# A two-layer encoder on one core: timeline-driven scheduling, TensorE in source order, later turns, all weight remainders on VectorE

## The chip, the cores and the metric

The kernel runs on one core of one Trainium2 chip. The metric is the device time of one execution in microseconds. The core has TensorE (PE in the rows; its weight loads are PEld), VectorE (DVE), ScalarE (ACT), GpSimd (POOL) and SyncE (SP), each with its own queue of instructions; they meet at semaphores.

## What is computed

x is 256 tokens by 1024 channels in float32, and there are two layers. In each, with RMSNorm ahead of every sublayer:

```python
for l in range(DEPTH):
    h_res = h_res + 0.5 * swiglu(rmsnorm(h_res, ffn1_norm[l]), ffn1_w_gate[l], ffn1_w_up[l], ffn1_w_down[l])
    z = rmsnorm(h_res, mix_norm[l]) @ w_in[l]
...
    y_att = dilated_attention(zq, zk, zv, q_norm[l], k_norm[l], biases)
    y_pool = pool_mixer(zp, pool_w[l], pool_scale[l])
    y_rec = hgrn2_bidirectional(hq, hi, hff, hfb, hg, lb_all[0, l], lb_all[1, l], hgrn_norm[l])
    h_res = h_res + jnp.concatenate([y_att, y_pool, y_rec], axis=-1) @ w_out[l]
    h_res = h_res + 0.5 * swiglu(rmsnorm(h_res, ffn2_norm[l]), ffn2_w_gate[l], ffn2_w_up[l], ffn2_w_down[l])
```

The attention has 8 heads of 64, the pooling 4 groups, and the recurrence (a gated scan over the tokens in both directions) 4 heads of 64. The FFN is 2816 wide.

## The kernel before

**Weights.** All weights stream in one after the other as 328 halves of 128x1024 float32 (512 KB each), each by one DMA on SP into one of 4 `stage` buffers. A product of float32 accuracy is made of three fp32r matmuls (`mm3`, `mm3t`, L164 to L176): every operand is split into a rounded part and a remainder. For a half `split_part` (L142) makes `whi` with an ACT copy and `wlo` with a subtraction; the subtraction runs on DVE, or on POOL for the 35 halves of the two mixers that `POOL_HALVES` lists (`on_pool`, L153). `ahead` (L158) starts the split of the half that lies LOOK = 4 further on. Activations are split alike by `split` (L256) and, for the normalised x, by `parts` (L270) into `xh` and `xl`.

**Stages.** There are six: FFN, mixer, FFN, twice. An FFN (`ffn`, L322) has 11 blocks; a block multiplies by 4 halves of gate and up (`gate_up`, L189), makes `h` with ACT and DVE, turns it with four TensorE transposes (`hp`, L352), and multiplies the block before by 2 halves of the down matrix (`down`, L238). At the end of a stage the four quarters of the new x are added (L371), squared on ACT for the norm (`squares`, L278), and turned by transposes (`turn`, L289, tiles `xps`) for the next stage; `to_stage` (L374) turns three at once and holds the last one back as `pending`, which `late_turn` (L183) issues inside the next stage.

**Mixer.** `mixer` (L449) first makes the gates `ga` and `gb` (`proj_pair`, 4 halves), then runs a list of steps by name, `ORDER[l]` (L48). `c:0` to `c:19` are the halves of the input projection (two for `hq`, four each for `q`, `k` and `zh`, two for `hg`, four for `v`). `ga`, `gb`, `uv` prepare the recurrence's `U` and `W`; its levels are `mm:m` (small TensorE matmuls, `lev`, L541), `put:m` (their results into `A`, for m below 32 a DVE copy by a mask, L566) and `up:m` (DVE multiplies U and W up to the next level, L520). `mm:m` needs the `U` and `W` that `up:m` left. `ns`, `nq`, `nk` scale and turn q and k, `sc`, `tr`, `pv` are the attention, `band` and `pool` the pooling, `join`, `rec`, `rnorm` end the recurrence, and `o:` are the four parts of the output projection (`wo`, 2 halves each). `head_rs` (L601) sums squares over a head with two matmuls `hss` for `rnorm`. Short-lived tiles of 128x512 come from a pool `t2` of T2 = 10 buffers.

**Order.** The tile scheduler orders the instructions of each engine by its priorities, which follow the source; only SP is in source order. So TensorE's order is the scheduler's.

**Start.** The kernel takes x twice: as it is and transposed (`xt_in`). The transposed copy lands in `self.xt0` by four DMAs on SP, between which the first half of weights comes in two parts; `body` makes `xh` and `xl` from it with no transpose. `setup` (L390) loads the masks and the bias table and builds the attention bias; it stands at block 4 of the first FFN.

Of the kernel before, what the change touches and what calls it, by code (L numbers as in the profile page):

```python
# [8 lines left out]
F32 = mybir.dt.float32  # L9
# [3 lines left out]
ALU = mybir.AluOpType  # L13
# [40 lines left out]
    ),  # L54
    (
# [7 lines left out]
POOL_HALVES = ((3, 4, 5, 7, 8, 9, 12, 16, 20, 22, 24, 25, 27, 28, 29, 31), (2, 5, 6, 7, 8, 12, 16, 18, 19, 20, 21, 23, 24, 25, 26, 27, 28, 29, 31))  # L63
T2 = 10
# [6 lines left out]
class Trunk:  # L71
    def __init__(self, ctx, tc, x_in, xt_in, wall, prm_in, rel_in, cst_in, cst2_in, msk_in, band_in, y_out):
# [18 lines left out]
        self.pending = None  # L91
# [11 lines left out]

        self.xt0 = self.bias[:, 0]
        self.cp.tile([P, 16], F32, name="pad0")
        xr = xt_in.rearrange("p (k t) -> p k t", k=KC)
# [3 lines left out]
        for j in range(4):  # L110
            if j < 2:
                q = slice(j * HALF // 2, (j + 1) * HALF // 2)
                nc.sync.dma_start(w0[:, q], wall[0][:, q])
            nc.sync.dma_start(self.xt0[:, 2 * j:2 * j + 2, :], xr[:, 2 * j:2 * j + 2, :])
        self.feed_dma(2)
        self.prm_in, self.cst_in = prm_in, cst_in
        self.ident = self.cst[:, K_ID:K_ID + P]
        nc.scalar.dma_start(self.ident, cst_in[:, K_ID:K_ID + P])
        nc.scalar.dma_start(self.x, x_in.rearrange("p (t d) -> p t d", t=2))
# [22 lines left out]
    def split_part(self, i, c0, c1):  # L142
# [40 lines left out]
    def late_turn(self):  # L183

        if self.pending is not None:
            self.pending()
            self.pending = None

    def gate_up(self, i0, gu, mid=None):  # L189

        for q in range(4):
            if q == 1:
                self.late_turn()
            if q == 2 and mid is not None:
                mid()
            self.ahead(i0 + q)
# [125 lines left out]
    def ffn(self, stage, post):  # L322
# [67 lines left out]
    def setup(self, after):  # L390
# [562 lines left out]
```

## Time and profile before

| | us |
|---|---|
| median of 3 runs | 1041.35 (1040.72 to 1043.3) |
| the profiled execution | 1040.81 |
| its span in the trace | 1039.0 |
| TensorE busy, share of the span | 1004.4 (97%) |
| VectorE busy | 585.0 (56%) |
| ScalarE busy | 538.8 (52%) |
| GpSimd busy | 88.3 (8%) |

Some 1.8 us of the profiled execution lie outside its span. A busy engine is one with an instruction in flight; a waiting instruction is not busy, and the idle time ahead of it is shown in brackets with what ended it. The six stages follow one another at 201.76, 333.67, 521.44, 708.60 and 849.72 us, where the first matmul of the next stage starts; the two mixers are the stretches from 201.76 to 333.67 and from 708.60 to 849.72.

### The profile page before, as it was taken

To read this page: it belongs to the slowest core of one execution; us is meant where nothing else is said; L and a number is where in the kernel's file an instruction comes from. 1 tells how busy PE (TensorE), PEld (TensorE's weight loads), DVE (VectorE), ACT (ScalarE), POOL (GpSimd) and SP (SyncE) were. 2 spreads that over 40 slices of the span, in tenths; PEclk is the share of its full clock that TensorE was granted. 3 is DMA by queue.
4 is the path that set the end of the run, shared out by engine and by line. 5 is a ranking of instruction groups with operands and counts; after the bars stand their busy time and mean duration, and the time that the engine had idled before them with its cause. 6 is when DMAs were issued, how large, how long until landed. Compare 5 with 4: busy or idle time off the path is not lost.

```text
span 1039.0 us, 14421 instructions
## 1 busy us (share of the span) xinstructions
PE 1004.4 (97%) x5682; PEld 826.2 (80%) x5682; DVE 585.0 (56%) x776; ACT 538.8 (52%) x774; POOL 88.3 (8%) x43
## 2 busy tenths in 40 slices
PE   6999999998999999999999999999889999999998
PEld 4878888886867888888878888889768678888886
DVE  5655555669835555555565555554977155555553
ACT  7544444684865544444564444447648555444442
POOL 0000000140230000000000000004132400000000
PEclk9999999999999999999999999999989999999999
DMA  7769655553334555555555555554523346555551
GB/s 265 245 219 329 234 188 193 165 163 123 103 122 136 179 192 182 186 192 188 185 168 187 190 185 186 195 185 138 165 83 102 102 147 196 184 185 189 194 186 58
DMA packets 50420, 182.20 MB, mean 175 GB/s; under 512 B 5768, under 2 KB 6024, under 8 KB 49968
## 3 DMA queue, kind: packets, MB, share of 16 engines
q1 hardware_dynamic: 48528, 174.09, 51.6%
q0 software_dynamic: 720, 4.21, 1.1%
q10 hardware_dynamic: 1104, 2.99, 0.8%
q8 instruction: 44, 0.72, 0.3%
q14 instruction: 24, 0.20, 0.1%
HBM read 180.20 MB, written 3.16 MB: 176 GB/s over the span
## 4 chain that ended last, share of the span: by engine, by line
PE 87%; DVE 6%; ACT 3%; issue 3%; DMA 1%; POOL 0%; SPq 0%; ACTq 0%; DVEq 0%; POOLq 0%
PE gu L175 15%; PE gu L176 15%; PE gu L174 15%; PE ya L174 8%; PE ya L176 8%; PE ya L175 8%; PE hp L352 2%; PE wo L174 2%; PE wo L175 1%; PE wo L176 1%; ACT whi L149 1%; DVE wlo L151 1%; PE xps L296 1%; DMA bias<-x_t 1%; PE lev L541 1%
## 5 line engine op out<-in xcount | busy, mean ns | idle before, releaser
L149 ACT ACTIVATE whi<-stage 128x1024 fp32r<-128x1024 f32 (+1 forms) x329 | 347.1, 1056 | 395.3 <-PE gu L176 202.3
L151 DVE TENSOR_TENSOR wlo<-stage,whi 128x1024 fp32r<-128x1024 f32 (+1 forms) x294 | 360.7, 1229 | 337.5 <-ACT whi L149 337.4
L174 PE MATMUL gu<-whi,xh 128*128 128x512 f32 x704 | 275.7, 392 | 8.0 <-ACT xh L274 5.7
L175 PE MATMUL gu<-wlo,xh 128*128 128x512 f32 x704 | 274.9, 391 | 0.5 <-DVE wlo L151 0.5
L176 PE MATMUL gu<-whi,xl 128*128 128x512 f32 x704 | 274.7, 390 | 0.0
L174 PEld LDWEIGHTS gu<-whi,xh 128*128 128x128 f32 x704 | 132.5, 188 | 37.5 <-ACT xh L274 5.7
L175 PEld LDWEIGHTS gu<-wlo,xh 128*128 128x128 f32 x704 | 132.7, 189 | 28.7 <-DVE wlo L151 1.4
L176 PEld LDWEIGHTS gu<-whi,xl 128*128 128x128 f32 x704 | 132.6, 188 | 27.7
L174 PE MATMUL ya<-whi,hi 128*128 128x512 f32 x352 | 141.2, 401 | 0.0
L151 POOL TENSOR_TENSOR wlo<-stage,whi 128x1024 fp32r<-128x1024 f32 x35 | 85.0, 2437 | 654.5 <-ACT whi L149 639.2
L176 PE MATMUL ya<-whi,lo 128*128 128x512 f32 x352 | 137.8, 391 | 0.0
L175 PE MATMUL ya<-wlo,hi 128*128 128x512 f32 x352 | 137.4, 390 | 0.0
L176 PEld LDWEIGHTS ya<-whi,lo 128*128 128x128 f32 x352 | 66.1, 188 | 14.3
L175 PEld LDWEIGHTS ya<-wlo,hi 128*128 128x128 f32 x352 | 66.3, 188 | 12.4
L174 PEld LDWEIGHTS ya<-whi,hi 128*128 128x128 f32 x352 | 66.2, 188 | 12.3
L345 ACT ACTIVATE g<-gu,rc 128x256 f32<-128x256 f32 x88 | 41.5, 475 | 47.4 <-PE gu L176 47.4
L346 DVE SCALAR_TENSOR_TENSOR h<-gu,rc,g 128x256 f32<-128x256 f32 x88 | 42.0, 481 | 23.7 <-ACT g L345 23.7
L260 DVE TENSOR_TENSOR lo<-hp,hi 128x512 fp32r<-128x512 f32 x44 | 30.1, 684 | 2.8 <-ACT hi L259 2.8
L259 ACT ACTIVATE hi<-hp 128x512 fp32r<-128x512 f32 x44 | 25.6, 581 | 2.7 <-PE hp L352 2.7
L541 PE MATMUL lev<-U,W 64*64 64x64 f32 x384 | 15.6, 237 | 11.4 <-DVE W L520 11.4
L352 PEld LDWEIGHTS hp<-cst,h 128*128 128x128 f32 x176 | 21.8, 139 | 5.7
L352 PE MATMUL hp<-cst,h 128*128 128x128 f32 x176 | 26.3, 272 | 0.0
(224 smaller groups left out, 1035.8 us busy)
## 6 DMA issues: line engine op xcount, KB each, us to landing
stage<-w_all SPq DMA_DIRECT2D x327, 512.0 KB, 3.5
skew<-drow POOLq DMA_DIRECT2D x1, 2048.0 KB, 12.1
bias<-skew POOLq DMA_DIRECT2D x2, 1024.0 KB, 10.3
bias<-x_t SPq DMA_DIRECT2D x4, 256.0 KB, 7.9
x<-x ACTq DMA_DIRECT2D x1, 1024.0 KB, 8.4
band<-band ACTq DMA_DIRECT2D x1, 1024.0 KB, 8.0
y_t<-x SPq DMA_DIRECT2D x4, 256.0 KB, 2.2
stage<-w_all SPq DMA_DIRECT2D x2, 256.0 KB, 4.7
```

The lines of the kernel that those rows point to most:

```text
L149: nc.scalar.activation(hi[:, s], st[:, s], AF.Copy)
L151: eng.tensor_tensor(lo[:, s], st[:, s], hi[:, s].bitcast(F32), op=ALU.subtract)
L174: nc.tensor.matmul(out, lhsT=ah, rhs=wh, start=start, stop=False, skip_group_check=True)
L175: nc.tensor.matmul(out, lhsT=ah, rhs=wl, start=False, stop=False, skip_group_check=True)
L176: nc.tensor.matmul(out, lhsT=al, rhs=wh, start=False, stop=stop, skip_group_check=True)
L259: self.nc.scalar.activation(hi, src, AF.Copy)
L260: self.nc.vector.tensor_tensor(lo, src, hi.bitcast(F32), op=ALU.subtract)
L296: nc.tensor.transpose(self.xps[k // 2][:, j % 2, tt * P:tt * P + P], self.x[:, tt, k * P:k * P + P], self.ident)
L345: silu = nc.scalar.activation(g2[:, tt, :], gu[tt][:, 0:256], AF.Silu, scale=r)
L346: nc.vector.scalar_tensor_tensor(h[:, tt, :], gu[tt][:, 256:512], r, g2[:, tt, :], op0=ALU.mult, op1=ALU.mult)
L352: nc.tensor.transpose(hp[:, f, tt * P:tt * P + P], h[:, tt, f * P:f * P + P], self.ident)
L541: nc.tensor.matmul(ps[d][e * 64:e * 64 + 64, hb * 64:hb * 64 + 64], lhsT=a, rhs=c, start=(hb == 0), stop=(hb == 7), skip_group_check=True)
```

## The change

1. The tile scheduler orders instructions with a simulated timeline (`schedule_with_timeline_sim`), and TensorE, like SP, is kept in source order.
2. `POOL_HALVES` and `on_pool` go: all subtractions for `wlo` are on DVE. 16 move in the first mixer and 19 in the second.
3. `ORDER` is rewritten: the levels are spread wider over the projections (in the first mixer `mm:2` from `c:6` to `c:7`, `mm:16` from `c:10` to `c:12`, `mm:128` from `c:13` to `c:15`), `rnorm` becomes `rn1` (squares and their split) and `rn2`, and `rec`, `rn1`, `rn2` come before the end of the projections. `ga`, `gb`, `uv` and `up` are given high priority.
4. `t2` has 16 buffers for 10; the `Kp` tag has one for two.
5. `to_stage` holds every turn back by one quarter.
6. The transposed copy of x is no longer an input. x comes by four DMAs on SP, 12 matmuls on a tile of ones stand at the start, and x is turned by 16 transposes, of which eight come in the second quarter of the first block; the squares come in its last quarter, and `look` grows from 0 to LOOK.
7. `setup` is cut in two: its loads stand at block 3, its computing at block 6.

```diff
-        "rnorm c:17 tr:6 tr:7 c:18 c:19 o:pool pv:0 pv:1 pv:2 o:rec pv:3 o:a0 o:a1 "
...
+        "c:14 mm:64 up:128 put:64 sc:2 tr:0 c:15 mm:128 put:128 join tr:1 sc:3 c:16 tr:2 band rec rn1 c:17 rn2 tr:3 tr:4 pool c:18 tr:5 tr:6 "
+        "c:19 tr:7 o:pool pv:0 pv:1 o:rec pv:2 pv:3 o:a0 o:a1 "
...
-T2 = 10
+FIRST = 400
+T2 = 16
...
-        eng = nc.gpsimd if self.on_pool(i) else nc.vector
-        eng.tensor_tensor(lo[:, s], st[:, s], hi[:, s].bitcast(F32), op=ALU.subtract)
-
-    def on_pool(self, i):
...
+        nc.vector.tensor_tensor(lo[:, s], st[:, s], hi[:, s].bitcast(F32), op=ALU.subtract)
...
-        self.feed_split(i + LOOK)
+        self.feed_split(i + self.look)
...
+            self.look = min(self.look + 1, LOOK)
...
+            if q == 3 and self.then is not None:
+                self.then()
+                self.then, self.look = None, LOOK
...
-            if b == min(4, NB - 1) and stage == 0:
-                self.setup(silu)
+            if b == 3 and stage == 0:
+                self.setup_loads(silu)
+            if b == 6 and stage == 0:
+                self.setup()
...
-            if (dh, tt) == (1, 1):
-                self.pending = lambda: self.turn(stage, dh, tt)
-            else:
-                self.turn(stage, dh, tt)
+            self.late_turn()
+            self.pending = lambda: self.turn(stage, dh, tt)
...
+        def rec_squares():
+            sq = self.t2("sq")
+            nc.scalar.activation(sq, V["ops"], AF.Square)
+            V["osq"] = self.split(sq)
...
-            do[nm](*([int(arg) if arg.isdigit() else arg] if arg else []))
+            with self.tc.high_priority(offset=FIRST) if nm in ("ga", "gb", "uv", "up") else nullcontext():
+                do[nm](*([int(arg) if arg.isdigit() else arg] if arg else []))
...
+        idle = self.pg.tile([P, 512], F32, tag="g", name="idle")
+        for _ in range(12):
+            self.nc.tensor.matmul(idle[:, 0:P], lhsT=self.ones, rhs=self.ones, start=True, stop=True)
+        for j in range(2):
+            self.split_part(0, j * HALF // 2, (j + 1) * HALF // 2)
         self.n_split = 1
...
+        for tt in range(2):
+            self.turn(0, 0, tt)
+        self.feed_dma(5)
+
+        def second():
             for tt in range(2):
-                self.squares(0, dh, tt)
+                self.turn(0, 1, tt)
+
+        def sums():
+            for dh in range(2):
+                for tt in range(2):
+                    self.squares(0, dh, tt)
+
+        self.pending, self.then, self.look = second, sums, 0
...
-        ctx.enter_context(tc.manual_schedule(engines={mybir.EngineType.SP}))
+        ctx.enter_context(tc.manual_schedule(engines={mybir.EngineType.SP, mybir.EngineType.PE}))
...
-    with tile.TileContext(nc) as tc:
+    with tile.TileContext(nc, schedule_with_timeline_sim=True) as tc:
```

How instructions stand now, at three places (line numbers are those of each kernel's own file).

ScalarE at the start of the program, before. `whi<-stage 128x512` are the two parts of the first half, `xh` the rounded parts of x, `sq` the squares.

```order
L149 ACT_TABLE_LOAD
L149 ACTIVATE whi<-stage 128x512
L274 ACTIVATE xh<-bias,prm 128x256 x2
L149 ACTIVATE whi<-stage 128x512
L274 ACTIVATE xh<-bias,prm 128x256 x6
L149 ACTIVATE whi<-stage 128x1024 x2
L283 ACTIVATE sq,ss<-x 128x512 x4
L287 ACT_TABLE_LOAD
```

The same place in the changed kernel:

```order
L281 ACTIVATE sq,ss<-x 128x512 x2
L149 ACTIVATE whi<-stage 128x512 x2
L281 ACTIVATE sq,ss<-x 128x512
L272 ACTIVATE xh<-xps,prm 128x256 x2
L281 ACTIVATE sq,ss<-x 128x512
L285 ACT_TABLE_LOAD
L272 ACTIVATE xh<-xps,prm 128x256 x2
L149 ACTIVATE whi<-stage 128x1024
L305 ACTIVATE rc<-rc,cols 128x2
L149 ACTIVATE whi<-stage 128x1024 x2
L306 ACTIVATE rc<-rc 128x2
L149 ACTIVATE whi<-stage 128x1024
```

All four squares and the second table load now stand ahead of the first whole halves, and the second half of `xh` behind them.

VectorE in the second mixer, where the level after the first is made (`hs` are sums of squares of q, `U` and `W` the recurrence's operands, `A` its result, `zq` the scaled q, `wlo` weight remainders), before:

```order
L151 TENSOR_TENSOR wlo_6311<-stage_6156,whi_6310 128x1024
L644 TENSOR_REDUCE hs_6235<-sq_6243 128x8
L520 TENSOR_TENSOR U_6174<-U_6174,dw_6144 128x512
L520 TENSOR_TENSOR W_6175<-W_6175,dw_6144 128x512
L651 TENSOR_TENSOR zq_6236<-zq_6236,hs_6235 128x512
L651 TENSOR_TENSOR zq_6241<-zq_6241,hs_6235 128x512
L566 COPY_PREDICATED A_6267<-msk_86,lev_6269 128x512
L566 COPY_PREDICATED A_6267<-msk_86,lev_6270 128x512
L151 TENSOR_TENSOR wlo_6368<-stage_6181,whi_6367 128x1024
```

The same place in the changed kernel:

```order
L150 TENSOR_TENSOR wlo_6362<-stage_6212,whi_6361 128x1024
L650 TENSOR_REDUCE hs_6266<-sq_6274 128x8
L569 COPY_PREDICATED A_6298<-msk_86,lev_6320 128x512
L523 TENSOR_TENSOR U_6205<-U_6205,dw_6175 128x512
L523 TENSOR_TENSOR W_6206<-W_6206,dw_6175 128x512
L569 COPY_PREDICATED A_6298<-msk_86,lev_6321 128x512
L657 TENSOR_TENSOR zq_6267<-zq_6267,hs_6266 128x512
L657 TENSOR_TENSOR zq_6272<-zq_6272,hs_6266 128x512
L150 TENSOR_TENSOR wlo_6391<-stage_6230,whi_6390 128x1024
```

The scaled q now stands behind both copies into `A`.

TensorE in the first mixer where the second matmul of the head sums `hss` stands, before (`pv` and `wo` are the attention's last product and the output projection, `v` the last input projection):

```order
L176 MATMUL wo<-whi,yl 128x512
L721 MATMUL pv<-PT,va 64x256 x7
L607 MATMUL hss<-lo,bones 128x512
L721 MATMUL pv<-PT,va 64x256 x5
L174 MATMUL wo<-whi,hi 128x512
L175 MATMUL wo<-wlo,hi 128x512
```

The same matmul in the changed kernel:

```order
L170 MATMUL v<-whi,xl 128x512
L609 MATMUL hss<-hi,bones 128x512
L610 MATMUL hss<-lo,bones 128x512
L715 MATMUL tp<-cst,P 128x128 x8
L751 MATMUL pps<-pm,prm 128x256 x2
L168 MATMUL v<-whi,xh 128x512
```

It has moved from inside the output projection to between two halves of `v`.

## Rows read from the trace of the kernel before

**Rows 1.** Engine table by stage: first mixer, the FFN after it, second mixer.

```profile
core 0: us, PE busy (x) PEld busy (x) DVE busy (x) ACT busy (x) POOL busy (x), PEclk, DMA share, GB/s
201.76:333.67 131.91, 124.08 (x1147) 102.25 (x1146) 87.75 (x166) 83.82 (x151) 36.31 (x15) 1.00 0.41 131
333.67:521.44 187.77, 186.99 (x855) 154.37 (x854) 102.95 (x113) 91.61 (x120) 0.00 (x0) 1.00 0.58 185
...
708.60:849.72 141.12, 129.89 (x1152) 107.31 (x1149) 86.16 (x156) 85.30 (x154) 43.91 (x18) 0.95 0.38 123
```

**Rows 2.** TensorE's waits, whole program: us in total, times, longest.

```profile
PE lev L541 <- DVE W L520: 11.4, 5, 4.5
PE gu L174 <- ACT xh L274: 5.7, 1, 5.7
PE wo L174 <- ACT hi L259: 4.5, 2, 2.2
PE xps L296 <- DVE x L371: 3.7, 5, 0.8
...
PE bps L405 <- DMA rel<-rel: 0.7, 1, 0.7
```

**Rows 3.** Timeline (start, us, what, [idle before]), second mixer, VectorE, GpSimd, TensorE.

```profile
763.75 1.85 DVE L520 TENSOR_TENSOR U<-U,dw 128x512 f32<-128x512 f32 x1
765.52 2.82 DVE L520 TENSOR_TENSOR W<-W,dw 128x512 f32<-128x512 f32 x1
...
765.44 2.35 POOL L151 TENSOR_TENSOR wlo<-stage,whi 128x1024 fp32r<-128x1024 f32 x1 [0.40 <-ACT whi L149]
...
768.49 0.37 PE L541 MATMUL lev<-U,W 64*64 64x64 f32 x2 [4.55 <-DVE W L520]
```

**Rows 4.** Engine table of the stretch behind that wait (columns as Rows 1).

```profile
768.00:772.00 4.00, 3.51 (x68) 3.13 (x69) 3.55 (x7) 0.00 (x0) 0.00 (x0) 0.50 0.47 144
```

**Rows 5.** VectorE's wait for a buffer, and TensorE's timeline in the second output projection.

```profile
DVE lo L260 <- PE pv L721: 22.7, 2, 14.4
...
824.75 0.66 PE L174 MATMUL wo<-whi,hi 128*128 128x512 f32 x1 [2.23 <-ACT hi L259]
```

**Rows 6.** Groups by line (busy us, mean ns), and two rows of VectorE's timeline.

```profile
L151 DVE TENSOR_TENSOR wlo<-stage,whi 128x1024 fp32r<-128x1024 f32 (+1 forms) x294 | 360.7, 1229 | 337.5 <-ACT whi L149 337.4
...
L566 DVE COPY_PREDICATED A<-msk,lev 128x512 f32<-128x512 uint8 x20 | 14.7, 734 | 0.7 <-PE lev L541 0.5
...
L151 POOL TENSOR_TENSOR wlo<-stage,whi 128x1024 fp32r<-128x1024 f32 x35 | 85.0, 2437 | 654.5 <-ACT whi L149 639.2 <-DVE A L566 15.3
...
227.84 3.46 DVE L510 TENSOR_TENSOR W<-q,dw 64x1024 f32<-64x1024 f32 x1
...
236.88 0.68 DVE L520 TENSOR_TENSOR U<-U,dw 128x512 f32<-128x512 f32 x1
```

**Rows 7.** TensorE's timeline at the end of the first FFN.

```profile
200.17 0.40 PE L176 MATMUL ya<-whi,lo 128*128 128x512 f32 x1
201.35 0.66 PE L296 MATMUL xps<-cst,x 128*128 128x128 f32 x4 [0.78 <-DVE x L371]
```

**Rows 8.** Timeline of the start, ScalarE and TensorE.

```profile
10.26 2.50 ACT L274 ACTIVATE xh<-bias,prm 128x256 fp32r<-128x256 f32 x6 [1.25 <-DMA bias<-x_t]
...
5.75 0.80 PE L174 MATMUL gu<-whi,xh 128*128 128x512 f32 x1 [5.75 <-ACT xh L274]
...
10.81 0.63 PE L174 MATMUL gu<-whi,xh 128*128 128x512 f32 x1
11.24 0.63 PE L175 MATMUL gu<-wlo,xh 128*128 128x512 f32 x1
...
15.02 0.50 PE L175 MATMUL gu<-wlo,xh 128*128 128x512 f32 x1 [0.53 <-DVE wlo L151]
...
28.33 0.39 PE L176 MATMUL gu<-whi,xl 128*128 128x512 f32 x1
28.56 0.60 PE L352 MATMUL hp<-cst,h 128*128 128x128 f32 x4
```

More of the change, by code (lines that the diff above doesn't have):

```diff
@@ L1 @@
-from contextlib import ExitStack
+from contextlib import ExitStack, nullcontext
 import numpy as np
@@ L71, with __init__ @@
 class Trunk:
-    def __init__(self, ctx, tc, x_in, xt_in, wall, prm_in, rel_in, cst_in, cst2_in, msk_in, band_in, y_out):
+    def __init__(self, ctx, tc, x_in, wall, prm_in, rel_in, cst_in, cst2_in, msk_in, band_in, y_out):
         self.tc, self.nc = tc, tc.nc
@@ L90, in __init__ @@
         self.cur = 0
-        self.pending = None
+        self.pending = self.then = None
+        self.look = LOOK
         self.x = self.cp.tile([P, 2, D], F32, name="x")
@@ L101, in __init__ @@
         self.qgs = self.cp.tile([P, 8], F32, name="qgs")
-        self.xt0 = self.bias[:, 0]
-        self.cp.tile([P, 16], F32, name="pad0")
-        xr = xt_in.rearrange("p (k t) -> p k t", k=KC)
+        xr = x_in.rearrange("p (t d) -> p t d", t=2)
+        self.ident = self.cst[:, K_ID:K_ID + P]
+        nc.scalar.dma_start(self.ident, cst_in[:, K_ID:K_ID + P])
         nc.scalar.dma_start(self.prm[:, 0:C_PW], prm_in[:, 0:C_PW])
@@ L109, in __init__ @@
         self.n_dma = 1
[L110 to L114, printed above, removed]
+        for dh in range(2):
+            s = slice(dh * 512, dh * 512 + 512)
+            for tt in range(2):
+                nc.sync.dma_start(self.x[:, tt, s], xr[:, tt, s])
+            if dh == 0:
+                for j in range(2):
+                    q = slice(j * HALF // 2, (j + 1) * HALF // 2)
+                    nc.sync.dma_start(w0[:, q], wall[0][:, q])
         self.feed_dma(2)
         self.prm_in, self.cst_in = prm_in, cst_in
-        self.ident = self.cst[:, K_ID:K_ID + P]
-        nc.scalar.dma_start(self.ident, cst_in[:, K_ID:K_ID + P])
-        nc.scalar.dma_start(self.x, x_in.rearrange("p (t d) -> p t d", t=2))
         self.bones = self.cp.tile([P, P], F32R, name="bones")
@@ L387, in out_part, with setup_loads @@
         self.nc.sync.dma_start(yr[:, tt, s], self.x[:, tt, s])
-    def setup(self, after):
+    def setup_loads(self, after):
         nc = self.nc
@@ L401, in setup @@
             nc.scalar.dma_start(self.band, self.band_in.rearrange("p (g s t) -> p g s t", g=4, s=2))
+        self.later = cst2, rel, mskf
+    def setup(self):
+        nc = self.nc
+        cst2, rel, mskf = self.later
         nc.vector.tensor_copy(self.msk, mskf)
@@ L577, in lev_put @@
             else:
-                V["Ao"] = tl("Kp", [P, 8, P], bufs=2)
+                V["Ao"] = tl("Kp", [P, 8, P])
                 for d in range(2):
@@ L604, in head_rs @@
             f = lambda t: t.rearrange("p a t -> p (a t)")
-            hi, lo = self.split(sq)
+            hi, lo = sq
             nc.tensor.matmul(ps, lhsT=self.bones, rhs=f(hi), start=True, stop=False)
@@ L796, in mixer @@
             "nk": lambda j: qk_turn("k", j), "sc": att_scores, "tr": att_tr, "pv": att_pv, "rec": rec_mm,
-            "rnorm": rec_norm, "o": out,
+            "rn1": rec_squares, "rn2": rec_norm, "o": out,
         }
@@ L806, in body @@
         self.new_xt()
-        for j in range(4):
-            if j < 2:
-                self.split_part(0, j * HALF // 2, (j + 1) * HALF // 2)
-            for k in (2 * j, 2 * j + 1):
-                self.parts(0, k, self.xt0[:, k, :])
+        idle = self.pg.tile([P, 512], F32, tag="g", name="idle")
+        for _ in range(12):
+            self.nc.tensor.matmul(idle[:, 0:P], lhsT=self.ones, rhs=self.ones, start=True, stop=True)
+        for j in range(2):
+            self.split_part(0, j * HALF // 2, (j + 1) * HALF // 2)
         self.n_split = 1
-        self.feed_split(2)
-        for dh in range(2):
+        for tt in range(2):
+            self.turn(0, 0, tt)
+        self.feed_dma(5)
+        def second():
             for tt in range(2):
-                self.squares(0, dh, tt)
+                self.turn(0, 1, tt)
+        def sums():
+            for dh in range(2):
+                for tt in range(2):
+                    self.squares(0, dh, tt)
+        self.pending, self.then, self.look = second, sums, 0
         for l in range(DEPTH):
@@ L941 @@
     inp = {k: np.asarray(v) for k, v in inputs.items()}
-    x, xt, wall, prm = _pack(inp)
+    x, wall, prm = _pack(inp)
     cst, cst2, msk, band = _constants()
-    arrays = dict(x=x, x_t=xt, w_all=wall, params=prm, rel=np.ascontiguousarray(inp["rel_bias"]), cst=cst, cst2=cst2, msk=msk, band=band)
+    arrays = dict(x=x, w_all=wall, params=prm, rel=np.ascontiguousarray(inp["rel_bias"]), cst=cst, cst2=cst2, msk=msk, band=band)
     nc = bacc.Bacc("TRN2", target_bir_lowering=False, num_devices=1)
```

12 lines of the change are left out of this document (3 added, 9 removed), and 13 rows, old and new, of the table ORDER.

## Prediction, made before the changed kernel was run

> **What bounds the kernel now.** I read first the table of engines by stage, to see where TensorE is not full. The FFN after the first mixer is: 186.99 us busy of 187.77 [rows 1]. The mixers are not: 7.83 us of the first are without a matmul (131.91 less 124.08), and the second takes 9.21 us more for the same work, at a mean granted clock of 0.95 [rows 1]. VectorE is busy 67% of the first mixer (87.75 of 131.91) [rows 1], so TensorE sets the end, and what can be had is where it waits.
>
> Next the list of TensorE's waits, to see who ends them. The largest is `lev`, the recurrence's small matmuls, on VectorE's `W`: 11.4 us in five waits; then 5.7 us at the start, 4.5 us at two `wo` matmuls, 3.7 us at five turns of x, 0.7 us at the bias table [rows 2].
>
> Third the timeline around the longest wait. `lev` at 768.49 stood idle for 4.55 us; `U` and `W` of that step took 1.85 and 2.82 us while a subtraction ran on GpSimd [rows 3], and the same operation takes 0.68 us where GpSimd is still [rows 6]. So VectorE and GpSimd slow one another. Behind the wait the granted clock was 0.50, the lower of the two levels, 1.2 GHz [rows 4]. This costs the second mixer 5.8 us of busy time (129.89 against 124.08 for the same matmuls) [rows 1], 2.9 us for each of its two long waits.
>
> Last, the `wo` waits. `lo<-sq` on VectorE waited 22.7 us in two places for `pv` on TensorE [rows 5], which is no input of it: it wants a `t2` buffer. The head sum comes late for that, and `wo` stands 2.23 us at 824.75 [rows 5].
>
> **The change part by part.** The sum goes against the profiled execution, 1040.8 us, 0.5 us under the median of the runs.
>
> *Mixers.* TensorE's work there doesn't change. At full clock and without idle time a mixer is 124.1 us, the busy time of the first [rows 1]; two are 248.2, and before they took 273.0 [rows 1]. So 24.8 us can be had, if everything goes.
>
> What goes. The steps of the recurrence stand further apart on TensorE and `up` is first on VectorE, so of the 11.4 us [rows 2] most goes. 16 buffers and the earlier `rn1`, `rn2` take away the wait for a buffer, and with it the 4.5 us [rows 2]: the head sum now stands ahead of the last halves of `v`. The slow clock goes with the waits that it follows, 5.8 us less what new waits bring.
>
> What comes. 35 subtractions of 1.229 us go to VectorE: 43.0 us [rows 6]. Against it GpSimd no longer slows VectorE. From the rows beside GpSimd this gives back 1.85 + 2.82 less 2 x 0.68 = 3.3 us at that one level [rows 3, 6], and at `W` of the first mixer 3.46 less 1.23, what 1024 elements take elsewhere, = 2.2 us [rows 6]; I take 12 us over both mixers, an estimate (the bounds are the 5.5 us of these two places and the 16 us that three such places in each mixer would give). VectorE's net load grows by 31 us to 87.75 + 86.16 + 31 = 205 us, 83% of 248 [rows 1]. There is room, but little at the level steps, where VectorE has its queue full.
>
> With TensorE in source order each wait is now a stop with everything behind it. I walked the new order of TensorE, ScalarE and VectorE with durations of these rows. The worst place is `nq:0` of the second mixer, the turn of q. On VectorE stand, from the end of `c:6`: `wlo` 1.23, the sum of squares 0.68, a masked copy 0.73, `U` and `W` 0.68 each, a masked copy 0.73, two scalings of q of 0.68: 6.1 us (0.68 stands for each plain operation of 128x512) [rows 6]. TensorE has 12 matmuls of `c:7` in that time, 2.8 us at 0.23 each (28.33 to 28.56) [rows 8], and the level's own. The wait is between 0 and 3.3 us; I take 2.2, as the level's matmuls lie in the same time. The same walk puts VectorE 1.8 us late at level 64 there, and ScalarE 1.5 us late at `rec`, behind the copies into `Ao`; with 0.5 for small ones and 1 us of lower clock behind them the second mixer has 7. In the first mixer it leaves 3 us in five places of 0.4 to 0.8 each. Together 10, with bounds of 0 and of the 24.8 that are there now. Mixers: 248.2 + 10 = 258.2, that is **-14.8**.
>
> *Later turns.* At the end of the first FFN the last matmul starts at 200.17, is over in its 0.23 us of pace, and the turn starts at 201.35: 0.95 us lost [rows 7]. The turn waits for the addition just ahead of it. With the turn one quarter later, the six matmuls between (1.4 us) hide it. Two more FFN ends read alike, and five waits of this kind add up to 3.7 us [rows 2]; two of the five lie inside the mixers' stretches and are counted there. Three: between -2.2 (3 x 0.74) and -2.9 (3 x 0.95); **-2.6**. If the cover is gone, the 0.95 us come back.
>
> *Bias table.* Its loads stand three blocks ahead of its matmul: the 0.7 us [rows 2] go, **-0.7**. On GpSimd's queue its DMAs have the rest of the FFN.
>
> *Start.* The first `hp` turn, behind 72 matmuls, is at 28.56; at 0.23 us they are 16.6, so 12 us of delay stand ahead [rows 8]. Of these 5.75 are until the first matmul, the rest is waits up to 15.02, and a slower pace: 0.43 us from 10.81 to 11.24, nearly the 0.45 of the lower clock level [rows 8]. Afterwards x comes whole, by the same SP queue, ahead of the weights; both versions need the same bytes for the first quarter but for one part of x more. ScalarE still has the same conversions, with four squares and a table load now ahead of the whole halves. The first block ends on ScalarE's chain in both. I take **0**. Lower bound: if the 12 matmuls on ones bring the clock up, the 12 first matmuls save 0.2 each, -2.4. Upper: if the eight `xh` conversions, 0.42 each (2.50 for six [rows 8]), stand uncovered in the chain, +3.3.
>
> For the rule on this there is "TensorE: Matmul & The Clock Gate" of the Trainium skill: its Part 1 says that the throttled state is the default and activity releases it, and its Part 4 that transposes do not count as busy in the same way. By the first the start would give -2.4, the sum 1020; by the second the eight transposes ahead undo a part of it, and the start gives 0. No row here has transposes alone, so this decides nothing.
>
> Sum: 1040.8 - 14.8 - 2.6 - 0.7 + 0 = **1022.7**, so 1023.
>
> **The rivals.**
>
> *VectorE becomes the mixers' bound (1037.5).* The 43 us land where VectorE has its queue full; level steps wait as long as before, only for `wlo` in the place of slow `W`s. The mixers keep 273.0, and only the ends of stages and the bias table gain: 1040.8 - 3.3 = 1037.5. For it: 3.55 us of 4 busy on VectorE behind the level step [rows 4]. Against: 83% over the whole, and a fast `W` of 0.68. Chance 0.14.
> The Trainium skill's "Perfetto Trace Analysis", in Identifying the Most-Contended Engine, ranks engines by occupancy; by that rule TensorE stays first in the mixers, and the trace agrees.
>
> *Slower (1057).* TensorE in source order stops at a level step as long as at 768.49, 4.55 us [rows 3], and is at the lower clock behind it, 2.9 us: 7.4 us. Three of these in each mixer make 124.1 + 22.3 = 146.4 us each, 292.8 together, and 1040.8 + 19.8 - 3.3 = 1057. It decides from the point where waits and clock cost the mixers over 24.8 + 3.3 = 28.1 us. For it: the scheduler no longer fills TensorE's waits with later matmuls. Against: the levels have been spread, with 12 matmuls or more between most. Chance 0.07.
>
> *All waits vanish (1011).* Mixers at 248.2, and the start at -2: 1040.8 - 24.8 - 3.3 - 2 = 1010.7. For it: no one of my waits is over 2.2 us, each the difference of two long sums. Chance 0.14.
>
> *The order does no more than the old one (1041).* The chosen order of VectorE puts halves ahead of `up` in spite of its priority. The rows of the order speak against it. Chance 0.03.
>
> **How the numbers follow.** The forecast, 1023, has 0.62, over some 1016 to 1031 (waits of 3 to 18 us in the mixers). For 8 in 10 the range takes the nearer halves of the two neighbours: 1011 to 1037. About 0.3%, 3.1 us, can be told from no change, so 1037.5 lies on its edge: of that rival's 0.14 I give 0.09 to faster and 0.05 to same. Faster 0.62 + 0.14 + 0.09 = 0.85; same 0.05 + 0.03 = 0.08; slower 0.07.
>
> **What would show it.** In the stage table of the changed kernel the mixers at 126 to 132 us each, VectorE busy near 103 in each and GpSimd near 0; `W` at 0.68 everywhere; no `lo` waiting for `pv`; no turn of x in TensorE's list; the `hp` turn of the first block near 28.6. Wrong would be: `lev` waits over 10 us in sum, a granted clock under 1 in the first mixer, waits of `gu` or `v` for `wlo` (VectorE the bound), or a first `hp` turn later than 32 us.

## The result, and the profile after

The changed kernel takes 1031.41 us (median of 4 runs, 1030.87 to 1032.17) against 1042.26 us for the kernel before in the same comparison. The ratio is 0.9898, with a 95% interval of 0.9881 to 0.9915: 1.0% faster, where 1.7% was forecast. The profiled execution took 1031.32 us with a span of 1029.5, 9.5 us under that of before. It is taken apart here by stage; a stage runs from its own first matmul to that of the next, and the first FFN is cut at its first `hp` turn.

| us | before | changed | difference | forecast |
|---|---|---|---|---|
| up to the first `hp` turn | 28.56 | 31.40 | +2.84 | 0 |
| rest of the first FFN | 173.20 | 172.47 | -0.73 | -0.7 (bias table) and its share of the turns |
| first mixer | 131.91 | 127.05 | -4.86 | |
| second FFN | 187.77 | 188.21 | +0.44 | |
| third FFN | 187.16 | 188.23 | +1.07 | |
| second mixer | 141.12 | 132.38 | -8.74 | both mixers -14.8 |
| last FFN | 189.28 | 189.76 | +0.48 | turns -2.6 in all |

The mixers gave 13.6 us, close to the forecast. The later turns gave nothing, and the start lost. The stage rows that answer to [rows 1], of the changed kernel (columns: busy time and instructions of each engine, granted clock of TensorE, DMA):

```profile
core 0: us, PE busy (x) PEld busy (x) DVE busy (x) ACT busy (x) POOL busy (x), PEclk, DMA share, GB/s
...
203.87:330.92 127.05, 123.02 (x1144) 102.59 (x1144) 96.63 (x181) 83.84 (x150) 0.00 (x0) 1.00 0.42 133
330.92:519.13 188.21, 187.18 (x852) 154.49 (x853) 103.14 (x113) 91.67 (x119) 0.00 (x0) 1.00 0.59 185
...
707.36:839.74 132.38, 125.42 (x1145) 103.69 (x1145) 96.53 (x173) 84.83 (x150) 0.00 (x0) 0.99 0.40 128
```

GpSimd is at 0 in the mixers, and VectorE has risen by 8.9 and 10.4 us, 19.3 together and not 31. TensorE's waits, which answer to [rows 2]:

```profile
PE gu L168 <- ACT xh L272: 4.5, 2, 2.8
PE tp L666 <- DVE zq L657: 3.3, 4, 2.1
PE gu L168 <- DVE xl L273: 2.2, 3, 0.7
PE ga L161 <- DVE xl L273: 1.5, 2, 0.7
PE xps L294 <- DVE x L371: 1.5, 5, 0.3
...
PE lev L552 <- DVE W L523: 0.8, 1, 0.8
PE wo L168 <- ACT PT L717: 0.7, 1, 0.7
PE lev L544 <- DVE W L523: 0.4, 1, 0.4
```

The 11.4 us of `lev` have shrunk to 1.2, the 4.5 us of `wo` on the head sum and the bias table's 0.7 us are gone. New are `tp` on the scaled q (3.3 us), single waits of `pbs` and `sc` of 1.4 us each, not shown here, and, at each of the five stage ends, the next stage's first `gu` or `ga` on `xl` (3.7 us together). The turns `xps` still lose 1.5 us, for 3.7 before.

### The profile page after: what moved, and what is told of

It is laid out like the page before. It is cut to its first block, busy times and chain, and to the rows that moved or that the text cites. A ratio compares the mean times of both kernels' runs of the same rounds, so it can differ in the third digit from the quotient of the medians.

```text
span 1029.5 us, 14460 instructions
## 1 busy us (share of the span) xinstructions
PE 1005.6 (98%) x5722; PEld 830.7 (81%) x5722; DVE 608.0 (59%) x811; ACT 539.4 (52%) x774; POOL 3.3 (0%) x8
## 4 chain that ended last, share of the span: by engine, by line
PE 89%; DVE 6%; ACT 3%; issue 1%; DMA 1%; SPq 0%; ACTq 0%
PE gu L168 16%; PE gu L170 16%; PE gu L169 16%; PE ya L170 8%; PE ya L168 8%; PE ya L169 8%; PE hp L352 2%; DVE wlo L150 2%; ACT whi L149 1%; PE wo L168 1%; PE wo L170 1%; PE wo L169 1%; PE xps L294 1%; PE pv L727 1%; DVE A L569 1%
## 5 line engine op out<-in xcount | busy, mean ns | idle before, releaser
L150 DVE TENSOR_TENSOR wlo<-stage,whi 128x1024 fp32r<-128x1024 f32 (+1 forms) x329 | 401.6, 1222 | 356.9 <-ACT whi L149 356.1
L169 PEld LDWEIGHTS ya<-wlo,hi 128*128 128x128 f32 x352 | 66.3, 188 | 12.6
L272 ACT ACTIVATE xh<-xps,prm 128x256 fp32r<-128x256 f32 x48 | 20.6, 470 | 6.7 <-PE xps L294 3.5
L273 DVE SCALAR_TENSOR_TENSOR xl<-xps,prm,xh 128x256 fp32r<-128x256 f32 x48 | 21.5, 479 | 3.7 <-ACT xh L272 3.4
```

The source lines that it names most:

```text
L150: nc.vector.tensor_tensor(lo[:, s], st[:, s], hi[:, s].bitcast(F32), op=ALU.subtract)
L169: nc.tensor.matmul(out, lhsT=ah, rhs=wl, start=False, stop=False, skip_group_check=True)
L272: nc.scalar.activation(self.xh[:, k, :], src, AF.Copy, scale=g)
L273: nc.vector.scalar_tensor_tensor(self.xl[:, k, :], src, g, self.xh[:, k, :].bitcast(F32), op0=ALU.mult, op1=ALU.subtract)
```

## The experiments

The theory taken into them was the prediction's: the spread steps with TensorE in source order carry the mixers' gain, and taking GpSimd out is a smaller part. The rival was that VectorE and GpSimd slowing one another was itself the cost. The table has the two kernels and the twelve that were run beside them. Each was compared with the kernel before in its own series, whose median lay between 1042.25 and 1042.57 us; the stage times are from one profiled execution each, and "hp" is the first `hp` turn.

| kernel | median us | ratio to before (95%) | hp | first mixer | second FFN | second mixer |
|---|---|---|---|---|---|---|
| before | 1042.26 | 1 | 28.56 | 131.91 | 187.77 | 141.12 |
| changed | 1031.41 | 0.9898 (0.9881 to 0.9915) | 31.40 | 127.05 | 188.21 | 132.38 |
| dve_only | 1033.85 | 0.9920 (0.9894 to 0.9946) | 28.85 | 132.09 | 187.77 | 132.71 |
| pool_back | 1037.76 | 0.9955 (0.9935 to 0.9976) | 30.39 | 131.85 | 188.24 | 134.41 |
| old_order | 1045.35 | 1.0028 (1.0016 to 1.0041) | 30.25 | 136.54 | 188.23 | 137.81 |
| pe_manual | 1059.54 | 1.0170 (1.0142 to 1.0198) | 28.65 | 141.78 | 190.76 | 144.36 |
| dve_t2 | 1026.25 | 0.9851 (0.9823 to 0.9880) | 29.16 | 127.80 | 187.78 | 129.34 |
| nq_late | 1026.11 | 0.9847 (0.9825 to 0.9870) | 31.08 | 127.10 | 188.26 | 126.31 |
| half_lag | 1035.68 | 0.9937 (0.9916 to 0.9958) | 30.44 | 129.75 | 188.81 | 135.11 |
| late_pair | 1027.60 | 0.9865 (0.9831 to 0.9899) | 31.31 | 127.42 | 187.59 | 130.01 |
| old_start | 1029.62 | 0.9879 (0.9856 to 0.9903) | 28.52 | 127.01 | 188.15 | 132.19 |
| sq_late | 1032.86 | 0.9911 (0.9885 to 0.9937) | 33.18 | 128.59 | 188.22 | 130.95 |
| no_idle | 1030.05 | 0.9889 (0.9862 to 0.9916) | 31.77 | 128.58 | 188.26 | 129.38 |
| comb | 1021.13 | 0.9796 (0.9783 to 0.9809) | 29.79 | 127.81 | 187.56 | 125.56 |

### What carries the mixers' gain

**dve_only**: the kernel before, with the list of GpSimd's halves emptied.

```diff
-POOL_HALVES = ((3, 4, 5, 7, ...), (2, 5, 6, 7, ...))
+POOL_HALVES = ((), ())
```

> The kernel before with one part of the change alone: all weight remainders on VectorE, GpSimd makes none. Theory (the new order of the mixers' steps carries the gain): the mixers keep some 270 us of their 273, because 43 us more stand in VectorE's queue ahead of the level steps, though W takes 0.68 us each; 1037 to 1043 us. Rival (VectorE and GpSimd slowing one another was the cost): the mixers fall by 10 us or more, 1028 to 1032 us.

It gave 8.4 us, near the rival's range: one part of the change alone makes most of its gain. All of it lies in the second mixer. Its stage rows and TensorE's two largest mixer waits:

```profile
202.99:335.08 132.09, 125.51 (x1148) 103.56 (x1146) 96.89 (x181) 84.17 (x151) 0.00 (x0) 0.99 0.40 128
710.64:843.35 132.71, 125.45 (x1148) 103.55 (x1146) 96.14 (x173) 84.26 (x151) 0.00 (x0) 0.99 0.40 128
...
PE lev L541 <- DVE W L520: 7.3, 7, 1.9
...
PE wo L174 <- ACT hi L259: 4.5, 2, 2.2
```

No `lev` waits over 1.9 us now, where the longest was 4.55 [rows 3], and the second mixer's busy time falls from 129.89 [rows 1] to 125.45: the lower clock behind the long wait went with it. The first mixer, which had no wait of over 2.3 us, gained nothing.

**pool_back**: the changed kernel, with those 35 halves on GpSimd again.

```diff
+POOL_HALVES = (the lists of the kernel before)
...
-        nc.vector.tensor_tensor(lo[:, s], st[:, s], hi[:, s].bitcast(F32), op=ALU.subtract)
+        l, n = divmod(i, N_HALVES // DEPTH)
+        eng = nc.gpsimd if n - FFN_HALVES in POOL_HALVES[l] else nc.vector
+        eng.tensor_tensor(lo[:, s], st[:, s], hi[:, s].bitcast(F32), op=ALU.subtract)
```

> The changed kernel with the 35 remainders of the two mixers put back on GpSimd, the new order of steps kept. Theory (the order carries the gain): W and U are slowed again beside GpSimd, but the wider steps hide most of it; mixers 259 to 264 us for 259.4, 1031 to 1036 us. Rival (the contention was the cost): mixers back to 270 and more, 1042 us or more.

The mixers went up by 4.8 and 2.0 us, to 266.3: between the two. The total lost 6.4 us. `W` takes 836 ns in the mean again, for 684 in the changed kernel, and the `lev` waits are 3.9 us:

```profile
PE lev L547 <- DVE W L526: 3.9, 3, 2.0
...
L526 DVE TENSOR_TENSOR W<-W,dw 128x512 f32<-128x512 f32 x14 | 11.7, 836 | 0.0
```

So the spread list hides a part of the contention (the `lev` waits were 11.4 us [rows 2] with the old list), but taking GpSimd out is worth 6.8 us of mixers even there.

**old_order**: the changed kernel with the step lists of before.

```diff
-ORDER = (the lists of the changed kernel)
+ORDER = (the lists of the kernel before, rnorm as "rn1 rn2")
```

> The changed kernel with the two lists of steps of the kernel before (its rnorm as rn1 and rn2 one after the other). Theory (the spread of the levels is what makes source order on TensorE cheap): TensorE stops at the level steps, each stop with lower clock behind it; mixers 273 to 293 us, 1045 to 1065 us. Rival (TensorE's waits went with the contention and the buffers, the list matters little): mixers 259 to 264 us, 1031 to 1036 us.

The theory held at its low end: the mixers take 274.35 us, more than before, though nothing runs on GpSimd. TensorE stops in source order at the levels, at the turn of k behind the softmax and at the head sum:

```profile
PE lev L544 <- DVE W L523: 8.7, 6, 2.6
PE hss L609 <- ACT hi L257: 4.8, 2, 2.4
PE tp L666 <- DVE st L701: 4.4, 2, 2.2
```

**pe_manual**: the kernel before, TensorE in source order.

```diff
-        ctx.enter_context(tc.manual_schedule(engines={mybir.EngineType.SP}))
+        ctx.enter_context(tc.manual_schedule(engines={mybir.EngineType.SP, mybir.EngineType.PE}))
...
-T2 = 10
+T2 = 16
...
```

> The kernel before with TensorE in source order alone, and with the 16 buffers of t2 (and one of Kp) that it then needs. Theory: the old list of steps in source order stops TensorE at the level steps and, as no turn is held back, at three turns of x in each stage's end (0.9 us each); mixers 280 to 295 us, 1050 to 1070 us. Rival (the scheduler's order of TensorE was worth nothing): 1038 to 1043 us.

As expected: 17 us slower. (`Kp` has one buffer here, too.) The scheduler's order of TensorE was worth much, though not at the levels, whose 11.7 us are those of before (11.4 [rows 2]), but at the turns of x, where 15 waits replace five:

```profile
PE xps L296 <- DVE x L371: 16.3, 15, 1.7
PE lev L541 <- DVE W L520: 11.7, 5, 4.6
```

**dve_t2**: the kernel before with two parts of the change, VectorE alone and the 16 buffers.

```diff
-POOL_HALVES = ((3, 4, 5, 7, ...), (2, 5, 6, 7, ...))
-T2 = 10
+POOL_HALVES = ((), ())
+T2 = 16
...
```

> The kernel before with two parts of the change alone: all weight remainders on VectorE, and 16 buffers of t2 (one of Kp). Theory (the head sum's wait for a buffer costs two stops of wo of 2.23 us beside the contention): 1033.85 less 4.5, 1029.4 us, under the changed kernel without its new order. Rival (with the buffer there, the scheduler's TensorE stops elsewhere in the output projection): 1033 us.

This beats the changed kernel by 5 us. The `wo` waits are gone from TensorE's list, and the mixers take 257.1 us together. The changed kernel's take 259.4, and between 258.0 and 259.5 in the four kernels here that share its lists and its stage ends:

```profile
202.51:330.31 127.80, 123.18 (x1147) 102.09 (x1146) 96.86 (x181) 83.82 (x151) 0.00 (x0) 1.00 0.42 133
705.86:835.20 129.34, 124.46 (x1147) 103.27 (x1146) 96.35 (x173) 83.91 (x151) 0.00 (x0) 0.99 0.41 131
```

So two parts alone are enough for what the whole change gives in the mixers: they take 15.9 of the 24.8 us that could be had, and the lists, the priority and the source order as they stand in the change add nothing to that. The way there differs. With the old lists 7.3 us of `lev` waits stay, in this kernel as in dve_only; the new lists take them down to 1.2, but TensorE in source order then has 7.6 us of other waits in the mixers (`tp`, `sc`, `pbs`, `pps` and `wo`). The next run shows that the new lists can give more. The buffers alone, the timeline scheduling and the priority weren't tried by themselves.

**nq_late**: one step moved in the second mixer's list (the middle of one line of it).

```diff
-c:6 mm:1 up:2 put:1 c:7 nq:0 c:8 mm:2 up:4 nq:1
+c:6 mm:1 up:2 put:1 c:7 c:8 nq:0 mm:2 up:4 nq:1
```

> The changed kernel with one step moved: the first turn of q (nq:0) in the second mixer comes one half later, behind c:8. Theory (its 2.11 us wait, 0.36 behind it and the lower clock that follows are what the second mixer still loses): second mixer 127.5 to 128.5 us for 132.38, 1027 us. Rival (VectorE is behind by that much and the wait moves to the next level): second mixer 131 to 133 us, 1031 us.

The theory held: 5.3 us in the median, and the second mixer at 126.31 us, even under the expectation. Both mixers take 253.4 us, 3.7 less than in dve_t2. This is the wait that it removes, in the changed kernel (timeline of VectorE, TensorE, and the engine table of the stretch behind it):

```profile
744.29 0.67 DVE L523 TENSOR_TENSOR U<-U,dw 128x512 f32<-128x512 f32 x1
744.88 0.68 DVE L523 TENSOR_TENSOR W<-W,dw 128x512 f32<-128x512 f32 x1
745.47 0.72 DVE L569 COPY_PREDICATED A<-msk,lev 128x512 f32<-128x512 uint8 x1
746.09 1.28 DVE L657 TENSOR_TENSOR zq<-zq,hs 128x512 f32<-128x512 f32 x2
...
746.82 0.33 PE L666 MATMUL tp<-cst,zq 128*128 128x128 f32 x1 [2.11 <-DVE zq L657]
...
748.00:752.00 4.00, 4.00 (x13) 3.07 (x11) 1.47 (x3) 0.95 (x2) 0.00 (x0) 0.57 0.40 133
```

`U` and `W` are at 0.67 and 0.68 us, as hoped, but the scaling of q stands behind them and a masked copy. Behind the 2.11 us the granted clock is 0.57, most of that stretch at the lower level of 1.2 GHz.

### What the ends of the stages wait for

At the end of the first FFN, [rows 7] before, the changed kernel has (TensorE, then a row of VectorE):

```profile
198.14 0.39 PE L170 MATMUL ya<-whi,lo 128*128 128x512 f32 x1
198.82 0.66 PE L294 MATMUL xps<-cst,x 128*128 128x128 f32 x4 [0.29 <-DVE x L371]
...
202.54 0.60 PE L294 MATMUL xps<-cst,x 128*128 128x128 f32 x4
203.87 0.39 PE L161 MATMUL ga<-xh,whi 128*128 128x256 f32 x1 [0.74 <-DVE xl L273]
...
203.34 0.87 DVE L273 SCALAR_TENSOR_TENSOR xl<-xps,prm,xh 128x256 fp32r<-128x256 f32 x2
```

The turn still loses 0.45 us at its first place (198.14 and 0.23 to 198.82), and `ga` comes 0.98 us behind the four transposes of 202.54 (0.35 us). Together 1.43 us, for 0.95 before. `ga` starts as the first of the two `xl` of 203.34 ends.

**half_lag**: the second quarter's turn three matmuls earlier.

```diff
+                    if post is not None and (dh, tt, f) == (1, 0, 0):
+                        self.late_turn()
```

> The changed kernel with one turn of x per stage, that of the second quarter, placed 3 matmuls earlier (in the middle of the third quarter instead of at its end). Theory (the 0.98 us ahead of the next stage's first matmul is the chain turn, xh, xl of the second quarter): 0.6 to 0.7 us go at each of five ends, 1028 us, 3 to 3.5 us under the changed kernel. Rival (the turn then waits for its addition as long): within 1 us of the changed kernel's 1031.4.

Neither held: 4 us slower. `ga` starts 0.30 us behind the transposes (201.90 to 202.20), but the next tile, `gb`, stands 1.69 us. Its first product needs no more of x than that of `ga` did (the first part, k = 0), and it starts only when VectorE is through the last `xl` (204.24 and 0.48), which has come to stand behind a `wlo`; the profile names the small `rc` right behind that `xl`, which `gb` doesn't read:

```profile
202.90 0.28 PE L163 MATMUL ga<-xh,wlo 128*128 128x256 f32 x1
...
203.10 1.22 DVE L150 TENSOR_TENSOR wlo<-stage,whi 128x1024 fp32r<-128x1024 f32 x1 [0.36 <-ACT whi L149]
204.24 0.48 DVE L275 SCALAR_TENSOR_TENSOR xl<-xps,prm,xh 128x256 fp32r<-128x256 f32 x1
...
204.87 0.35 PE L161 MATMUL gb<-xh,whi 128*128 128x256 f32 x1 [1.69 <-DVE rc L305]
```

So the wait is not for data. The pool `pg` of the kernel, into whose tiles TensorE writes, has 4 buffers (banks of PSUM, its result memory); the turns ahead of the stage's end take all four for `xps`, and `ga` and `gb` then reuse the banks of the first two `xps`, which `xl` still reads. The kernel before has the same four banks taken there, and its scheduler puts even the held-back turn ahead of `ga`. But its `xl` come earlier: the second pair starts at 201.21, the first of it ends as the last turn does, and `ga` at 201.76 has nothing more to wait for:

```profile
201.21 0.87 DVE L275 SCALAR_TENSOR_TENSOR xl<-xps,prm,xh 128x256 fp32r<-128x256 f32 x2
```

**late_pair**: the last two turns both in the next stage, so that its first tiles find other banks.

```diff
-            self.late_turn()
-            self.pending = lambda: self.turn(stage, dh, tt)
+            if (dh, tt) == (1, 0):
+                return
+            self.late_turn()
+            if (dh, tt) == (1, 1):
+                self.pending = lambda: [self.turn(stage, 1, t) for t in range(2)]
+            else:
+                self.pending = lambda: self.turn(stage, dh, tt)
...
+                    if post is not None and (dh, tt, f) == (1, 0, 0):
+                        self.late_turn()
```

> The changed kernel with both turns of the last two quarters of x held back into the next stage, and the turn of the second quarter 3 matmuls earlier. Theory (the 0.74 us wait at each end is for a PSUM bank: with three turns ahead of the stage's end the next stage's first tiles get the banks of the first turn's xps, and wait for the last xl that reads them): the next stage's first tiles get free banks, the wait goes, FFN 2 at 187.2 to 187.5 us for 188.21, 1026 to 1027.5 us. Rival (the wait is for the data of x itself): FFN 2 stays at 188 to 188.8 us, 1030 to 1034 us.

The wait for `xl` is gone at all five ends, as the theory of the banks had it: `ga` follows the last matmul at pace.

```profile
202.18 0.39 PE L170 MATMUL ya<-whi,lo 128*128 128x512 f32 x1
202.41 0.28 PE L161 MATMUL ga<-xh,whi 128*128 128x256 f32 x1
```

The second FFN is 0.62 us shorter, the whole 3.8 us. That is less than 0.98 at each end, since the 0.29 us of `xps` at the first turn stays, and a few short waits come at the later transposes.

### What the start costs

The first block of the changed kernel, ScalarE and then TensorE ([rows 8] before):

```profile
8.70 0.82 ACT L272 ACTIVATE xh<-xps,prm 128x256 fp32r<-128x256 f32 x2
9.41 0.63 ACT L281 ACTIVATE sq<-x 128x512 f32<-128x512 f32 x1
...
10.15 1.28 ACT L285 ACT_TABLE_LOAD   x1
11.45 0.84 ACT L272 ACTIVATE xh<-xps,prm 128x256 fp32r<-128x256 f32 x2
...
5.37 1.04 PE L294 MATMUL xps<-cst,x 128*128 128x128 f32 x8
9.21 0.50 PE L168 MATMUL gu<-whi,xh 128*128 128x512 f32 x1 [2.80 <-ACT xh L272]
...
11.97 0.80 PE L168 MATMUL gu<-whi,xh 128*128 128x512 f32 x1 [1.74 <-ACT xh L272]
...
15.98 1.91 PE L294 MATMUL xps<-cst,x 128*128 128x128 f32 x8
```

The first transposes are done at 6.4 us, and TensorE then waits twice for `xh`, 2.80 and 1.74 us, with a square and a table load between the two pairs. Behind that its matmuls are 0.43 us apart.

**old_start**: the changed kernel with the start of before (the transposed x as an input, no matmuls on ones, no transposes).

```diff
...
-        self.pending, self.then, self.look = second, sums, 0
...
+        for j in range(4):
+            if j < 2:
+                self.split_part(0, j * HALF // 2, (j + 1) * HALF // 2)
+            for k in (2 * j, 2 * j + 1):
+                self.parts(0, k, self.xt0[:, k, :])
...
```

> The changed kernel with the start of the kernel before: transposed x as an input, no matmuls on ones, no transposes of x at the start, squares behind the third half's whi as they stood. Theory (the new start costs what its first hp turn is late, 31.40 against 28.56 us): hp at 28.6, 1028.6 us, 2.8 us under the changed kernel. Rival (the clock that the matmuls on ones bring is worth as much): hp at 28.6, but the first block's matmuls slower, 1031 us.

The first `hp` turn is at 28.52, as the theory had it; the profiled execution is 3.4 us shorter (1027.93), the median 1.8 us (1029.62; runs from 1027.93 to 1030.43). The first `hp` turn of one and the same start varies: 30.25 to 31.40 us in the six kernels of the table with the changed start, 28.52 to 29.79 in the six with that of before. So the start costs some 2 us, and the 2.84 of the two profiles lies at the high end.

**sq_late**: the squares and the table load behind the second half's `whi`.

```diff
...
-                    self.squares(0, dh, tt)
+                    with self.tc.issue_after(self.whi_at[1].ins):
+                        self.squares(0, dh, tt)
```

> The changed kernel with the four squares and the table load of the start held behind the whi of the second half on ScalarE, so that the first four xh conversions stand ahead of them. Theory (the second wait of gu for xh, 1.74 us, and part of the first, 2.80 us, are ScalarE's squares and table load): one wait goes, first hp turn at 29 to 29.8 us, 1029 to 1030 us. Rival (the 16 transposes and the lower clock are the whole loss): hp at 31, 1031 us.

The 1.74 us went, but the first `hp` turn came at 33.18, later and not earlier: the whole halves and the second half of `xh` are now behind the squares, and TensorE waits there.

```profile
8.39 0.50 PE L169 MATMUL gu<-whi,xh 128*128 128x512 f32 x1 [1.92 <-ACT xh L273]
...
20.23 0.50 PE L169 MATMUL gu<-whi,xh 128*128 128x512 f32 x1 [1.97 <-ACT xh L273]
```

So neither theory held as put. It looks as if the loss were ScalarE's whole chain in this stretch, and moving one piece of it moved the wait; no run here shortens the chain with the transposes kept.

**no_idle**: one matmul on ones for twelve.

```diff
-        for _ in range(12):
+        for _ in range(1):
```

> The changed kernel with 1 of the 12 matmuls on ones at the start. Theory (they end before x is there, and TensorE waits for xh behind them, so the lower clock comes all the same): first hp turn within 0.5 us of 31.40, 1031 us. Rival (they keep the first quarter of the block at the full clock): first hp turn 2 us and more later, 1033.5 us.

The `hp` turn came 0.37 us later, within the theory's 0.5. The median is 1.4 us lower all the same, which is not the start: in the profile the second mixer is 3.0 us shorter and had less of the lower clock (last section), while the first is 1.5 us longer. The twelve matmuls do change the pace of what follows at once, which the theory had not foreseen: without them the first eight transposes take 1.98 us, with them 1.04 (above). That this is lost in the two waits behind is not shown by itself, since the scheduler's order of ScalarE changed along with it: in no_idle the first `xh` stand between the squares and the halves (6.39 and 7.29 us), and the first `gu` comes earlier, at 7.44.

```profile
4.80 1.98 PE L294 MATMUL xps<-cst,x 128*128 128x128 f32 x8 [2.89 <-DMA cst<-cst]
7.44 0.79 PE L168 MATMUL gu<-whi,xh 128*128 128x512 f32 x1 [0.66 <-ACT whi L149]
```

### The edits together

**comb**: old_start, late_pair and nq_late in one kernel.

> The changed kernel with three edits tried alone: the start of the kernel before (old_start), both last turns held back (late_pair) and the first turn of q in the second mixer one half later (nq_late). Theory (they lie in different stages and add): first hp turn 28.5, first mixer 126.4, the two FFNs 187.6 each, second mixer 125.7 us; 1019 us. Rival (the two ends of a mixer and VectorE's fixed queue make them overlap): mixers as in the changed kernel, 1023 us or more.

1021.13 us (1020.75 to 1021.65), 2.0% under the kernel before and 10.3 us under the changed one, and the fastest here. It lies halfway between the two expectations. By stage the theory held better: the FFNs and the second mixer came as expected (187.56, 125.56), the first mixer 1.4 us and the first `hp` turn 1.3 us later than in the sum. By the medians the three edits nearly add: 1.8, 3.8 and 5.3 us alone, 10.9 in sum, 10.3 together. And it is 5.1 us under dve_t2: with its three weak places mended the whole change beats the two parts alone.

## Why the prediction came out as it did

The measured time lies in the range, on its slow side and just past the stretch of 1016 to 1031 that the forecast had for itself, 8.4 us over 1023 (9.5 us of gain in the profile for 18.1 us forecast). The mixers' term held; the misses are the later turns and the start. By the steps of the prediction:

- **Mixers, -14.8.** Measured -13.6 (259.43 us for 258.2). The walk of the orders was good where it was made: 2.11 us at `nq:0` for 2.2, and with the `nq` in the first mixer, `sc` on `Lk`, level 16 and `pps` five small waits that add up to 3.0 us, as forecast, if not at the same places. Level 64 came at 0.85 us for 1.8, `rec` didn't wait; `pbs` behind the softmax did, 1.44 us, unforeseen. So the sum came right in part by luck.
- **What goes, in the mixers.** This step is right on the `wo` waits and the buffers, and half right on the `lev` waits, which it put to the spread of the steps and to priority. They were 11.4 us before, 7.3 with GpSimd silent alone, 3.9 with the change but GpSimd working, 1.2 with all of it: the spread does shorten them. But the theory taken into the experiments, that it carries the mixers' gain, is refuted: dve_only and dve_t2 show GpSimd's silence and the buffers giving 15.9 us of mixers with the old lists and the scheduler's order. old_order shows what the spread is for: without it, source order on TensorE costs 14.9 us (274.35 for 259.43).
- **VectorE's load, +31.** Measured +19.3, and +19.1 in dve_only, where nothing else was changed. So the halves gave back some 24 us (43.0 less 19.3), over the upper bound of 16; 18.0 of them are seen directly, as the time by which VectorE's operations beside a subtraction were longer than the same operations in dve_only. The bound counted the slow `U` and `W` alone. Others were slow, too, as the operation on `dw` in `gates_a`, before and after:

```profile
L474 DVE SCALAR_TENSOR_TENSOR dw<-dw 128x1024 f32<-128x1024 f32 x2 | 4.0, 2013 | 4.4 <-ACT dw L473 4.4
...
L477 DVE SCALAR_TENSOR_TENSOR dw<-dw 128x1024 f32<-128x1024 f32 x2 | 2.5, 1225 | 0.1
```

  VectorE did not become the bound: it is busy 193.2 of the 259.4 us.
- **Later turns, -2.6.** This step failed. The cover that it named is there: six matmuls hide all but 0.29 us of the addition. But it took everything behind the turn to be as before. The turn of the second quarter, and `xl` behind it, come later too, and `xl` holds the banks that the next stage's first tiles reuse: 0.74 us of wait at each of five ends, where there was none. The other FFNs came to 0.44, 1.07 and 0.48 us more, some +2.0 in all for -2.6, so 4.6 us of the miss are here.
- **Bias table, -0.7.** Its wait is gone from TensorE's list. That the first FFN behind its first `hp` turn is 0.73 us shorter fits, though this stretch also holds the end that lost 0.48 more.
- **Start, 0.** Measured +2.84 (some 2 by the other runs, above), near the upper bound of +3.3, and for its reason: `xh` stands uncovered. This step failed, too. The 0 rested on the first block ending with ScalarE's chain in both kernels, without laying the new chain out in time against the old one. 2.8 us of the miss are here. The matmuls on ones do quicken, from 0.21 to 0.11 us apart at 4.25 us, and the eight transposes behind them take 1.04 us. This agrees with the rule of the Trainium skill ("TensorE: Matmul & The Clock Gate", Part 1) that activity releases the throttle. The start gained no time by it: waits of 2.80 and 1.74 us follow, and behind them the granted clock is 0.50 (12 to 16 us).
- **The rivals.** VectorE as the bound did not come. The slower one, 1057, did not come either. Source order without the spread, pe_manual, does reach such a time, 1059.54, but not by that rival's mechanism: the `lev` waits stayed as they were, and the turns of x lose 12.6 us more.

## What to carry to other kernels

When a change has several parts, each wait of the old profile belongs to one of them, and the cheap part should be run alone first: here two of them, one engine fewer and six buffers more, beat the whole change as it stood by 5 us, and the whole change came out ahead only when its three weak places had been found. Where an operation's duration differs by a factor of three between places, look for a neighbour that slows it, and go through all operations beside that neighbour, not only those that someone waits for: some are slowed and some are not. Before a step is moved later towards a stage's end, list which buffers it holds and who gets them next.

## What the runs showed of the hardware

- Some VectorE operations and GpSimd's subtractions took turns rather than sharing. In [rows 3] `W` starts at 765.52 beside a subtraction on GpSimd that runs from 765.44 to 767.79, and ends at 768.34, 0.55 us behind it; alone it takes 0.68. The 35 subtractions took 85.0 us on GpSimd [rows 6] and added only 19.3 us to VectorE. The operations that were slowed read SBUF, the memory of most of the kernel's tiles, alone (not every one that does was slowed); 40 that stood beside a subtraction and read a tile of PSUM kept their length, such as the additions `P<-sc,bias` of the softmax, 421 ns in the mean in 17 places beside one and in the 15 others:

```profile
283.69 2.38 POOL L151 TENSOR_TENSOR wlo<-stage,whi 128x1024 fp32r<-128x1024 f32 x1 [8.11 <-ACT whi L149]
283.92 0.42 DVE L695 CUSTOM_DVE_ANT_0 P<-sc,bias 128x256 f32<-128x256 f32 x1
```

  The Trainium skill's "SBUF — State Buffer", in SBUF: two separate sides, says that the two engines' common port pair is an exclusive lock, held for the whole instruction, and that it is taken by a VectorE operation in a two-port mode, or with two inputs in SBUF against a GpSimd operation that reads SBUF; the other engine blocks. The trace agrees, in the 2.82 us of `W` and in the 0.42 us of `P`. Weighed ahead of the prediction, the rule would have pointed at every such operation beside any of the 35, not at six places.
- The price of a short stop is not constant. The same wait of TensorE for `zq` took 2.11 us in the changed kernel, to 746.82, and 2.10 in no_idle, to 748.79. The stretches that begin 1.2 us behind it had a granted clock of 0.57 (shown at nq_late) and of 1.00, in no_idle:

```profile
750.00:754.00 4.00, 4.00 (x79) 3.14 (x78) 1.54 (x4) 2.01 (x3) 0.00 (x0) 1.00 0.39 134
```

  The second mixers are 132.38 and 129.38 us. So of the 6.1 us that nq_late takes from the second mixer about half may be this clock; each is one profiled execution. What decides between the two was not found.
- Transposes run at either pace: eight took 1.04 us behind busy matmuls, and 1.91 us at 15.98 in the changed kernel, where the granted clock is 0.50, the lower level. At the start of no_idle they took 1.98 us, though the profile has a granted clock of 1.00 there: over the first 10 us the pace says more of the clock than that column.
